# Two of eight depthwise convolution chunks moved from block matmuls to multiply-adds on VectorE

## The chip, the cores and the metric

One core of one Trainium2 chip runs the whole program. The metric is the device time of one execution in microseconds (us); of the kernel before there are three runs, and their median is compared with that of the changed kernel.

## What is computed

One layer of a hybrid decoder, in float32, for 256 prompt positions and 8 samples of 8 new positions (320 columns together, always in this order). The normalised input goes through one input projection (2048 to 3072). A third of its outputs are convolution values, a third are their gates, a third go to a state-space mixer (S5, then gelu and a sigmoid gate). The two mixers' outputs are normalised, projected, added to the input, and a SwiGLU feed-forward follows, then a last norm. The part that the change touches is the convolution of 1024 channels, cut here to its core:

```
u  = v * sigmoid(gate)                        # (b, l, 1024)
up = concatenate([conv_buf, u], axis=1)       # 30 earlier rows in front
y[t, c] = sum over k < 31 of up[t + k, c] * conv_w[k, c]   # each channel by itself
y  = y + conv_b                               # then LayerNorm over channels, swish
new_buf = up[:, -30:]
```

The prompt starts with 30 rows of zeros, each sample with its own 30 rows of state.

## The kernel before

**Weights.** All projections stream their weights in sub-steps of 256 rows by 512 columns. For each sub-step SyncE loads a tile `raw` (four buffers), ScalarE rounds it into `hi` (line 126), VectorE subtracts to get `lo` (line 127), and TensorE does 24 matmuls of 128x320 (lines 150 to 152: four output tiles, two row blocks, three products). `hi` and `lo` have three buffers.

**Order.** The kernel gives every piece of work a number with `when(slot)`: the sub-steps count 0, 1, 2, ..., and other work gets a slot among them, from the table `PLAN`. The framework lists the instructions of each engine in the order in which they become ready in its own simulated timeline, the lowest number first where several are ready, and each engine then runs its list in that order. An instruction that waits on the chip holds all that is behind it on its engine. Sub-steps 0 to 15 project the S5 inputs, 16 to 47 the convolution inputs: groups c0 to c3 of eight sub-steps, each of which gives two chunks of 128 channels, both values and gates. Sub-steps 48 to 55 are the projection `w_glu` of the S5 mixer, whose right side `gehl` comes from the gelu (lines 826 to 834), and this in turn from `yl`, 16 loads on SyncE's queue (line 821). After it come the output projection and the feed-forward.

**A convolution chunk.** When group ci ends, VectorE scales the projected values and gates (lines 915, 920), and writes their product into a window buffer `ubuf` (line 923). There are two such buffers, so that chunk c+2 can be written only when nothing reads chunk c any more. `conv_chunk` (from line 356) then loads the state rows `stn`, moves the samples' new columns (line 363), transposes the state rows on TensorE (line 367) and copies them into the window (ScalarE, line 368), and writes the new convolution state out (lines 370 to 374). After that the window is spread out: four transfers per chunk (line 378) copy it, shifted by 0, 8, 16 and 24 columns, into `ub`, 32 channels and four shifts on the 128 partitions. `conv_weights` (line 352, VectorE) builds block weights `cw` of 128x1024 from the taps. TensorE then does the convolution as 64 products over the prompt's columns (line 386, 128x256) and 64 over the samples' (line 390, 128x64), counted in the trace as instructions, into one PSUM tile `cx`, and ScalarE adds the bias (line 395). `ysum` on VectorE adds the chunk (line 399) for the LayerNorm at slot 62. `stn`, `cw`, `ub` and `cx` have one buffer each.

The slots of the chunks are `P_CONV`; `conv_chunk` is placed 2.2 before its entry and `conv_weights` 2.5 before, and the matmuls at the entry itself. The S5 outputs (`post`, lines 772 to 793) have slots 24 to 34.5, the S5 states 35, the gelu of block b has 44 + b/2.

Of the kernel before, what the change touches and what calls it, by code (L numbers as in the profile page):

```python
# [11 lines left out]
AF = mybir.ActivationFunctionType  # L12
OP = mybir.AluOpType
# [7 lines left out]
ORDER = (("s", 0), ("s", 1), ("c", 0), ("c", 1), ("c", 2), ("c", 3))  # L21
S0, S1 = (8 * ORDER.index(("s", i)) + 8 for i in range(2))
P_POST = [24, 25.5, 27, 28.5, 30, 31.5, 33, 34.5]
P_CONV = [27, 30, 35, 38, 43, 46, 51, 54]
P_GELU = 44
P_LN = 62
E_AT = {2: 0, 3: 1024}
# [12 lines left out]
           + ((("w", b + 2, P_POST[b] + 0.5),) if b < 6 else ())]  # L40
        + [("states", 0, P_POST[7] + 0.5), ("open_g", 0, P_POST[7] + 1)]
        + [("gelu", b, P_GELU + b / 2) for b in range(8)]
        + [("cw", b, P_CONV[b] - 2.5) for b in range(8)]
        + [("conv", b, P_CONV[b] - 2.2) for b in range(8)]
        + [("copy", 0, 65)])
P_RMIX = 0.58
SEQ = ("glu", "ssm", "conv")
# [8 lines left out]
def kernel(ctx: ExitStack, tc: tile.TileContext,  # L56
# [7 lines left out]
    V, A, G, T, SP = nc.vector, nc.scalar, nc.gpsimd, nc.tensor, nc.sync  # L64
# [3 lines left out]
    @contextmanager  # L68
    def when(slot):

        old = tc.cur_priority
        tc.cur_priority = int(BASE + slot * SLOT)
        yield
        tc.cur_priority = old
# [13 lines left out]
    def sx_tile(shape):  # L88
        return pss.tile(shape, F32, tag="sx", name="sx")

    def cx_tile(shape):
        return pss.tile(shape, F32, tag="cx", name="cx", bufs=1)
# [92 lines left out]
    convw = const.tile([128, 8, 32], F32, name="convw")  # L185
    G.memset(convw[:, :, 31:32], 0.0)

    def pv(i):
        return PV[:, i:i + 1]
    NMIX, NFFN, CB, LNG, LNB, GNC, GNS, SSD = 0, 16, 32, 40, 48, 56, 64, 72  # L190
# [6 lines left out]
    convy = convp.tile([128, 8, NTOK], F32, name="convy")  # L197
# [158 lines left out]
    def conv_chunk(c):  # L356
        u = us_.pop(c)
        traced.add(("conv", c))
        stn = convp.tile([120, 2, 128], F32, name="stn", bufs=1)
        SP.dma_start(stn, sc_dram[:, c * 128:(c + 1) * 128]  # L360
                     .rearrange("(h r) c -> r h c", h=2))
        win_ = u[:, 350:654].rearrange("p (b t) -> p b t", t=38)
        A.activation(win_[:, :, 30:38], u[:, 286:350].rearrange("p (b t) -> p b t", t=8), AF.Copy)
        pc = sx_tile([128, 368])
        ps = pc[:, 0:240].rearrange("p (h r) -> p h r", h=2)
        for h in range(2):
            T.transpose(ps[:, h, :], stn[:, h, :], ident[:120, :120])
        A.activation(win_[:, :, 0:30], ps.rearrange("p h (b t) -> p (h b) t", t=30), AF.Copy)
        ps = pc[:94, 240:368]
        T.transpose(ps, u[:, 256:350], ident)  # L370
        uo = convp.tile([94, 128], F32, name="uo", bufs=1)
        A.activation(uo, ps, AF.Copy)
        SP.dma_start(ncv_p[0, 0, :, c * 128:(c + 1) * 128], uo[0:30])
        SP.dma_start(ncv_s[0, :, 22:30, c * 128:(c + 1) * 128], uo[30:94])

        ub = convp.tile([128, 4, UW - 24], F32, name="ub", tag="wide")
        for b in range(4):
            SP.dma_start(ub[:, b, :],  # L378
                         bass.AP(tensor=u.tensor, offset=u[32 * b:32 * b + 32].offset,
                                 ap=[[u.ap[0][0], 32], [8, 4], [1, UW - 24]]))  # L380
        cw = cw_.pop(c)
        with when(P_CONV[c]):
            acc = cx_tile([128, NTOK])
            for k in range(8):
                for b in (3, 2, 1, 0):
                    T.matmul(acc[32 * b:32 * b + 32, 0:256], cw[:, b, k, :], ub[:, b, k:k + 256],  # L386
                             start=(k == 0), stop=False, skip_group_check=True)
            for k in range(8):
                for b in range(4):
                    T.matmul(acc[32 * b:32 * b + 32, 256:320].rearrange("p (b t) -> p b t", t=8),  # L390
                             cw[:, b, k, :],
                             bass.AP(tensor=ub.tensor, offset=ub[:, b, 350 + k:351 + k].offset,
                                     ap=[list(ub.ap[0]), [38, 8], [1, 8]]),
                             start=False, stop=(k == 7), skip_group_check=True)
            A.activation(convy[:, c, :], acc, AF.Identity, bias=pv(CB + c))
        if c == 0:
            V.tensor_copy(ysum, convy[:, 0, :])
        else:
            V.tensor_tensor(ysum, ysum, convy[:, c, :], op=OP.add)


    us = bigp.tile([128, 5248], F32, tag="h20", name="us")
# [325 lines left out]
    def s5_sample_states():  # L728
        assert all(("e", b) in traced for b in range(8))
        for h in range(2):  # L730
            scan_step(*((Sn[:, :, 8 * k:8 * k + 8], st0[:, :, 8 * k:8 * k + 8], *powers(0, k, 8))
                        for k in (2 * h, 2 * h + 1)))
# [428 lines left out]
    def post(b):  # L1161
# [4 lines left out]
    job(n_proj, open_mid)  # L1166
    parts_ = dict(v=pool_v, pre=pre, e=s5_e, w=pool_w, scan=s5_scan, post=post, gelu=gelu,
                  cw=conv_weights, conv=conv_chunk, sample=lambda b: s5_sample_states(),
                  states=lambda b: s5_states(), open_g=lambda b: open_g(),
                  copy=lambda b: SP.dma_start(ncv_s[0, :, 0:22, :], state_conv[0, :, 8:30, :]))  # L1170
# [66 lines left out]
```

## Time and profile before

| | us |
|---|---|
| median of three runs | 1435.41 (1434.61 to 1437.08) |
| the profiled execution | 1432.56 |
| its span, first to last instruction | 1430.8 |
| TensorE busy | 1387.2 (97%) |
| VectorE busy | 793.7 (55%) |
| ScalarE busy | 552.2 (39%) |

"Busy" of TensorE counts from the start of a matmul to its modelled end, and matmuls overlap: one of 128x320 is shown with 0.31 us, while the next starts 0.15 us behind it. So the pitch from start to start tells its cost. The same holds in a small way for VectorE, where the next instruction starts a little before the shown end of the one before. In a timeline row, the bracket at the end is the idle time of the engine ahead of that instruction and what ended it. PEclk is the clock granted to TensorE: 1.00 is 2.4 GHz, 0.50 is 1.2 GHz.

### The profile page before, as it was taken

What the parts mean: (1) busy time and instruction counts of PE and PEld (TensorE: products, weight loads), DVE (VectorE), ACT (ScalarE), POOL (GpSimd) and SP (SyncE); (2) the same over time, 40 slices, a digit from 0 to 9 for tenths busy, and PEclk for the clock granted to TensorE, in tenths of its full rate; (3) what the DMA queues carried; (4) which work ended last, traced back from release to release, by engine and by line L of the source; (5) the groups of instructions that cost most, each with busy time, mean ns of one, the idle gap of its engine ahead of it and who ended that gap; (6) DMA issues with size and microseconds to landing.
All of it is one profiled execution on the core that took longest, in us unless ns stands there. A gap on an engine that the chain in (4) does not pass through costs nothing.

```text
span 1430.8 us, 25250 instructions
## 1 busy us (share of the span) xinstructions
PE 1387.2 (97%) x10482; PEld 1354.9 (95%) x10482; DVE 793.7 (55%) x1400; ACT 552.2 (39%) x805; POOL 30.3 (2%) x61
## 2 busy tenths in 40 slices
PE   9999989799998999999999999999999999999995
PEld 8899978788998999999999999999999999999995
DVE  7778985365887744445434544443444435444465
ACT  7434434354464433333333332333333233332232
POOL 0121000000000000000000000000000000000000
PEclk9999999999999999999999999999999999999997
DMA  9874564966543444544444444445444444454432
GB/s 259 223 156 140 168 187 127 164 180 198 190 148 109 149 142 148 160 148 148 148 151 152 150 152 148 148 148 154 154 149 148 148 149 149 156 180 148 148 133 74
DMA packets 147739, 222.73 MB, mean 156 GB/s; under 512 B 32505, under 2 KB 57657, under 8 KB 147480
## 3 DMA queue, kind: packets, MB, share of 16 engines
q1 hardware_dynamic: 144488, 211.09, 48.5%
q0 software_dynamic: 3136, 10.03, 2.8%
q8 instruction: 82, 1.34, 0.4%
q14 instruction: 33, 0.27, 0.1%
HBM read 201.04 MB, written 10.41 MB: 148 GB/s over the span
## 4 chain that ended last, share of the span: by engine, by line
PE 88%; DMA 4%; DVE 3%; SPq 2%; ACT 2%; issue 1%; ACTq 0%; DVEq 0%
PE mm L151 27%; PE mm L152 27%; PE mm L150 27%; DMA ub<-ubuf 3%; PE cx L386 2%; SPq L378 1%; DMA raw<-in_w_in_dram 1%; DVE lo L127 1%; PE sx L787 1%; PE sx L782 1%; PE sx L689 1%; PE cx L390 0%; DMA yl<-yd 0%; DVE us L705 0%; ACT hi L126 0%
## 5 line engine op out<-in xcount | busy, mean ns | idle before, releaser
L127 DVE TENSOR_TENSOR lo<-raw,hi 128x1024 fp32r<-128x1024 f32 x352 | 430.5, 1223 | 449.9 <-ACT hi L126 449.2
L126 ACT ACTIVATE hi<-raw 128x1024 fp32r<-128x1024 f32 x352 | 372.9, 1060 | 653.2 <-PE mm L151 580.0
L150 PE MATMUL mm<-hn,hi 128*128 128x320 f32 x1408 | 434.8, 309 | 0.0
L151 PE MATMUL mm<-hn,hi 128*128 128x320 f32 x1408 | 434.7, 309 | 0.0
L152 PE MATMUL mm<-hn,lo 128*128 128x320 f32 x1408 | 431.1, 309 | 0.0
L150 PEld LDWEIGHTS mm<-hn,hi 128*128 128x128 f32 x1408 | 264.3, 188 | 0.1
L151 PEld LDWEIGHTS mm<-hn,hi 128*128 128x128 f32 x1408 | 264.3, 188 | 0.0
L152 PEld LDWEIGHTS mm<-hn,lo 128*128 128x128 f32 x1408 | 263.2, 188 | 0.0
L150 PE MATMUL mm<-aout,hi 128*128 128x320 f32 x704 | 217.3, 309 | 0.0
L151 PE MATMUL mm<-aout,hi 128*128 128x320 f32 x704 | 217.1, 309 | 0.0
L152 PE MATMUL mm<-aout,lo 128*128 128x320 f32 x704 | 214.7, 309 | 0.0
L150 PEld LDWEIGHTS mm<-aout,hi 128*128 128x128 f32 x704 | 132.2, 188 | 0.0
L151 PEld LDWEIGHTS mm<-aout,hi 128*128 128x128 f32 x704 | 132.2, 188 | 0.0
L152 PEld LDWEIGHTS mm<-aout,lo 128*128 128x128 f32 x704 | 131.5, 188 | 0.0
L151 PE MATMUL mm<-xhl,hi 128*128 128x320 f32 x384 | 121.2, 318 | 0.5 <-DVE xhl L257 0.5
L152 PE MATMUL mm<-xhl,lo 128*128 128x320 f32 x384 | 121.4, 319 | 0.0
L150 PE MATMUL mm<-xhl,hi 128*128 128x320 f32 x384 | 117.4, 319 | 3.5 <-ACT hi L126 2.7
L150 PEld LDWEIGHTS mm<-xhl,hi 128*128 128x128 f32 x384 | 71.8, 191 | 5.7 <-ACT hi L126 2.9
L151 PEld LDWEIGHTS mm<-xhl,hi 128*128 128x128 f32 x384 | 73.5, 192 | 1.7 <-DVE xhl L257 1.1
L152 PEld LDWEIGHTS mm<-xhl,lo 128*128 128x128 f32 x384 | 73.6, 192 | 1.1 <-issue 0.8
L1051 DVE TENSOR_TENSOR h<-mm,h 128x320 f32<-128x320 f32 x64 | 30.0, 487 | 41.2 <-PE mm L152 41.2
L386 PE MATMUL cx<-ub,cw 128*32 128x256 f32 x512 | 35.0, 382 | 10.9 <-DMA ub<-ubuf 10.9
(312 smaller groups left out, 1346.2 us busy)
## 6 DMA issues: line engine op xcount, KB each, us to landing
raw<-in_w_ffn_gate_dram SPq DMA_DIRECT2D x88, 512.0 KB
raw<-in_w_ffn_up_dram SPq DMA_DIRECT2D x88, 512.0 KB
raw<-in_w_ffn_down_dram SPq DMA_DIRECT2D x88, 512.0 KB
raw<-in_w_in_dram SPq DMA_DIRECT2D x64, 256.0 KB
raw<-in_w_out_dram SPq DMA_DIRECT2D x32, 512.0 KB
ub<-ubuf SPq DMA_DIRECT2D x32, 316.0 KB
raw<-in_w_in_dram SPq DMA_DIRECT2D x16, 512.0 KB
tst<-KTd POOLq DMA_DIRECT2D x8, 512.0 KB, 5.6
```

What stands on the lines that cost most here:

```text
L126: A.activation(hi, src, AF.Copy)
L127: V.tensor_tensor(lo, src, hi.bitcast(F32), op=OP.subtract)
L150: T.matmul(ps, wh, xh, start=(k == 0), stop=False)
L151: T.matmul(ps, wh, xl, start=False, stop=False)
L152: T.matmul(ps, wl, xh, start=False, stop=(k == g.nk - 1))
L378: SP.dma_start(ub[:, b, :], bass.AP(tensor=u.tensor, offset=u[32 * b:32 * b + 32].offset, ap=[[u.ap[0][0], 32], [8, 4], [1, UW - 24]]))
L386: T.matmul(acc[32 * b:32 * b + 32, 0:256], cw[:, b, k, :], ub[:, b, k:k + 256], start=(k == 0), stop=False, skip_group_check=True)
L689: T.matmul(ps[64 * g2:64 * g2 + 64, q, r, :], e[:, q, r, 64 * g2:64 * g2 + 64], uall[:, 8 * b + 2 * q + g2, :], start=True, stop=True)
L782: T.matmul(ps[:, 2 * q:2 * q + 2, :].rearrange("p g j -> p (g j)"), w[:, q, r].rearrange("p t c -> p (t c)"), hbd[:, q, r].rearrange("p g ...
L787: T.matmul(ps[:, g, :], t2[:, g].rearrange("p t c -> p (t c)"), uall[:, 8 * b + g, :], start=False, stop=(g == 7), skip_group_check=True)
L1051: V.tensor_tensor(h[:, n, :], ps, h[:, n, :], op=OP.add)
```

## The change

Chunks 3 and 5 get no block weights, no `ub` and no convolution matmuls. Their window is read where it stands: ScalarE writes the product of tap 0 plus the bias, and VectorE does 30 further multiply-adds in place, each as two instructions, prompt (128x256) and samples (128x64) in turn. Tap k of a chunk has the slot `P_CONV` + 0.2 k. The chunks' entries in `P_CONV` go from 38 to 34 and from 46 to 42, and for them `conv_chunk` is placed at the entry and not 2.2 before it. Loading of the state rows, window, transposes and state outputs stay.

```diff
-P_CONV = [27, 30, 35, 38, 43, 46, 51, 54]
+P_CONV = [27, 30, 35, 34, 43, 42, 51, 54]
+V_CONV = {3: 0.2, 5: 0.2}
...
-        + [("cw", b, P_CONV[b] - 2.5) for b in range(8)]
-        + [("conv", b, P_CONV[b] - 2.2) for b in range(8)]
+        + [("cw", b, P_CONV[b] - 2.5) for b in range(8) if b not in V_CONV]
+        + [("conv", b, P_CONV[b] - (0 if b in V_CONV else 2.2)) for b in range(8)]
...
+        if c in V_CONV:
+            return conv_taps_on_v(c, u, win_)
...
+    def conv_taps_on_v(c, u, win_):
+
+        pairs = [(convy[:, c, 0:256], lambda k: u[:, k:k + 256]),
+                 (convy[:, c, 256:320].rearrange("p (b t) -> p b t", t=8),
+                  lambda k: win_[:, :, k:k + 8])]
+        for dst, src in pairs:
+            A.activation(dst, src(0), AF.Identity, bias=pv(CB + c), scale=convw[:, c, 0:1])
+        for k in range(1, 31):
+            with when(P_CONV[c] + V_CONV[c] * k):
+                for dst, src in pairs:
+                    V.scalar_tensor_tensor(dst, src(k), convw[:, c, k:k + 1], dst,
+                                           op0=OP.mult, op1=OP.add)
+        with when(P_CONV[c] + V_CONV[c] * 31):
+            add_ysum(c)
```

`add_ysum` holds the two lines that add a chunk to `ysum`; the other chunks call it as before.

## Rows read from the trace of the kernel before

**Rows 1.** The page: TensorE's busy time and share of the span; granted clock by slice

```profile
PE 1387.2 (97%) x10482; PEld 1354.9 (95%) x10482; DVE 793.7 (55%) x1400; ACT 552.2 (39%) x805; POOL 30.3 (2%) x61
...
PEclk9999999999999999999999999999999999999997
```

**Rows 2.** The page's chain that ended last: share of the span by engine

```profile
PE 88%; DMA 4%; DVE 3%; SPq 2%; ACT 2%; issue 1%; ACTq 0%; DVEq 0%
```

**Rows 3.** TensorE's waits, 170 to 360 us: total us, times, longest

```profile
PE cx L386 <- DMA ub<-ubuf: 10.9, 7, 3.2
PE sx L370 <- ACT ubuf L368: 5.5, 1, 5.5
```

**Rows 4.** Timeline of TensorE around the convolution of chunks 3 and 5

```profile
266.98 3.69 PE L386 MATMUL cx<-ub,cw 128*32 128x256 f32 x64 [2.03 <-DMA ub<-ubuf]
...
271.55 0.42 PE L367 MATMUL sx<-ident,stn 120*128 120x120 f32 x2
...
271.96 0.30 PE L150 MATMUL mm<-xhl,hi 128*128 128x320 f32 x1
272.11 0.31 PE L151 MATMUL mm<-xhl,hi 128*128 128x320 f32 x1
...
281.39 0.45 PE L370 MATMUL sx<-ident,ubuf 128*94 128x128 f32 x1 [5.45 <-ACT ubuf L368]
...
281.90 0.47 PE L150 MATMUL mm<-xhl,hi 128*128 128x320 f32 x1
...
285.90 0.47 PE L150 MATMUL mm<-xhl,hi 128*128 128x320 f32 x1
286.72 0.40 PE L367 MATMUL sx<-ident,stn 120*128 120x120 f32 x2 [0.35 <-DMA stn<-in_state_conv_dram]
...
307.73 3.68 PE L386 MATMUL cx<-ub,cw 128*32 128x256 f32 x64 [2.25 <-DMA ub<-ubuf]
```

**Rows 5.** Timeline of VectorE: what follows a multiply-add, and when

```profile
125.13 0.33 DVE L662 SCALAR_TENSOR_TENSOR ks<-e,PV,cx 128x128 f32<-128x128 f32 x1
125.38 0.67 DVE L604 TENSOR_TENSOR vw<-pw,Bb 128x512 f32<-128x512 f32 x1
...
410.30 0.55 DVE L891 SCALAR_TENSOR_TENSOR half<-lnt,PV,half 128x320 fp32r<-128x320 f32 x1
410.76 0.49 DVE L959 TENSOR_TENSOR t<-mm,Rs 128x320 f32<-128x320 f32 x1
...
18.78 1.55 DVE L439 SCALAR_TENSOR_TENSOR prm<-prm 128x32 f32<-128x32 f32 x7
```

**Rows 6.** Busy us of PE, PEld, DVE, ACT, POOL, then PEclk, by stretch

```profile
230.00:260.00 30.00, 28.43 (x296) 25.23 (x295) 8.69 (x11) 12.81 (x28) 0.88 (x1) 1.00 0.48 137
260.00:300.00 40.00, 31.77 (x392) 28.12 (x391) 19.74 (x32) 19.01 (x45) 0.00 (x0) 0.91 1.01 194
...
230.00:330.00 100.00, 87.12 (x988) 78.38 (x990) 44.14 (x65) 43.91 (x94) 0.88 (x1) 0.97 0.75 169
```

**Rows 7.** VectorE's waits, 230 to 330 us: total us, times, longest

```profile
DVE cw L352 <- PE cx L390: 21.0, 3, 14.3
...
DVE ubuf L923 <- DMA ub<-ubuf: 4.6, 1, 4.6
```

**Rows 8.** VectorE's groups of instructions, 282 to 302 us: busy us, mean ns

```profile
L832 DVE TENSOR_TENSOR ge<-gz,yl 128x320 f32<-128x320 f32 x8 | 6.0, 774 | 0.0
...
L834 DVE TENSOR_TENSOR gehl<-ge,gehl 128x320 fp32r<-128x320 f32 x8 | 3.9, 497 | 0.0
L829 DVE TENSOR_TENSOR gz<-gsq,yl 128x320 f32<-128x320 f32 x8 | 3.9, 494 | 10.6 <-DMA yl<-yd 9.1 <-ACT gsq L827 1.5
L352 DVE TENSOR_TENSOR cw<-tapw,blkmask 128x1024 f32<-128x1024 f32 x1 | 1.2, 1236 | 0.0
```

**Rows 9.** Timeline of ScalarE behind chunk 3's bias, 270 to 282 us

```profile
280.60 0.47 ACT L826 ACTIVATE gsq<-yl 128x320 f32<-128x320 f32 x1 [8.37 <-DMA yl<-yd]
280.98 0.35 ACT L368 ACTIVATE ubuf<-sx 128x240 f32<-128x240 f32 x1
```

More of the change, by code (lines that the diff above doesn't have):

```diff
@@ L395, in conv_chunk, with add_ysum @@
             A.activation(convy[:, c, :], acc, AF.Identity, bias=pv(CB + c))
+        add_ysum(c)
+    def add_ysum(c):
         if c == 0:
@@ L399, in conv_chunk @@
             V.tensor_tensor(ysum, ysum, convy[:, c, :], op=OP.add)
+    def conv_taps_on_v(c, u, win_):
[10 more added lines that the diff above has]
+        with when(P_CONV[c] + V_CONV[c] * 31):
+            add_ysum(c)
     us = bigp.tile([128, 5248], F32, tag="h20", name="us")
```

## The prediction

> **What bounds the kernel now.** I read the page first: TensorE is busy 97% of the span, VectorE 55%, and the granted clock is at its upper level, 2.4 GHz, in every slice but the last [rows 1]. The chain of waits says the same: 88% of it is TensorE, 4% transfers, 3% VectorE [rows 2]. So the kernel is a stream of matmuls, and what TensorE need not do, or need not wait for, is gained, as long as the rest keeps up. I then looked for the places where the stream breaks. TensorE's waits between 170 and 360 us are two things: 10.9 us, in seven pieces, for the spread window `ub` ahead of convolution matmuls, and one wait of 5.5 us for a copy on ScalarE [rows 3]. TensorE's timeline places them [rows 4]: 2.03 us ahead of chunk 3, 2.25 us ahead of chunk 5, and 5.45 us at 276 to 281.4, after which the matmuls of 128x320 run for a while at 0.267 us from start to start (281.90 to 285.90 is 15 pitches), not at 0.15 as at 271.96: the clock had fallen to 1.2 GHz. The stretch table has the mean of 0.91 there [rows 6].
>
> **TensorE's work that goes.** Chunk 3's matmuls occupy TensorE from 266.98 to 271.55, when the next instruction starts: 4.57 us [rows 4]. Chunk 5's first burst is as long (3.68 us against 3.69), so 4.57 again: 9.14 us together. Nothing replaces this on TensorE, and it is on the bound: gain 9.1.
>
> **Waits that go with it.** The two waits for `ub` directly ahead, 2.03 and 2.25, go too: gain 4.3 [rows 4]. What is late next is only what TensorE needs anyway, `hi` and `lo` of the next sub-step. Their lead is two sub-steps, 2 x 24 matmuls x 0.15 = 7 us, from which a rounding on ScalarE and a subtraction on VectorE, near 1 us each, are to be taken. Four issues on SyncE's queue and four transfers go per chunk as well; TensorE's list of waits has none for weights [rows 3], so I count them at nothing, hidden behind the matmuls.
>
> **What VectorE gets.** Per chunk 30 pairs of multiply-adds, with a per-partition factor. The trace has that form at 128x128: 125.13, next start 125.38, so 0.25 us; and at 128x320: 410.30 to 410.76, 0.46 us [rows 5]. That is 0.21 / 192 = 1.09 ns a column; at 256 columns it makes 0.25 + 128 x 0.00109 = 0.39, at 64 columns 0.25 - 0.07 = 0.18. A pair is 0.57 us, 30 are 17.1, both chunks 34.2 us. Each step needs the one before of its own kind. The one chain of that sort, seven of 128x32, took 1.55 us, 0.22 each, though one alone is shown with under 0.2: with such a wait the pitch is about the full shown length [rows 5]. Prompt and samples in turn put the other instruction into that gap. If nothing were hidden, a pair would be 0.48 + 0.28 (the shown lengths 0.33 and 0.55 put on the same line) = 0.76, and both chunks 46 us. I take 34, since the alternation fits that gap; the upper end stays for the range. The block weights go: 1.2 us each [rows 8], so net +32 us.
>
> The Trainium skill ("VectorE: DVE Perf Modes", section "The DRAIN you can't avoid") says that the next operation does not start until the pipe of the one before is empty, and that one should hold the number of operations down; that speaks against 120 small ones. By the row it is not so in this kernel: the next one started 0.46 us into an operation shown with 0.55 [rows 5]. By the page's sentence the sum would be the 46 us, by the row the 34.
>
> **Is there room?** Between 230 and 330 us VectorE is busy 44.1 of 100 us, between 230 and 260 only 8.7 of 30, between 260 and 300 19.7 of 40 [rows 6]. With the 32 us it would be busy 76 of a stretch that shrinks to 87 us. Chunk 3's steps have slots 34.2 to 40, after nearly all of the S5 outputs; its `conv_chunk` goes from slot 35.8 to 34, ahead of the last S5 output and of the states. So its window should stand near 236, not at 256, and 17 us of steps lie in a stretch with 21 us free, much of it a wait for the weights' buffer `cw` (14.3 us at once [rows 7]) which this chunk no longer makes. Chunk 5's product into `ubuf` waits for the last step of chunk 3; before it waited for the `ub` transfer until 267 (4.6 us [rows 7]), so I count nothing. Chunk 5's steps, slots 42.2 to 48, meet the gelu (44 to 47.5), 13.8 us on VectorE [rows 8]. The stretch 260 to 300 then holds 19.7 + 17.1 - 1.2 = 35.6 of 40 us: full, but not over.
>
> **What I can't size.** (a) The hole at 276: ScalarE stood 8.37 us for `yl` with chunk 4's window copy right behind in its list [rows 9]; both come near in other order once chunk 3 is off SyncE's queue. Its price is 5.45 idle, 16 slow matmuls x 0.12 = 1.9, and 0.35 behind them: 7.7. The change gives back 0 to 7.7; I take 2.6, a third, because `yl` keeps its rank in the table. (b) New stalls: a step standing at the head of VectorE's list holds the `lo` or the PSUM reads behind it. From 0 to what would be left over if chunk 3's steps fell into 260 to 300 as well: 35.6 + 17.1 - 40 = 12.7. I take 2.6, near the lower end, since the stretch row has the room.
>
> **Sum.** 9.1 + 4.3 + 2.6 - 2.6 = 13.4 us off the profiled execution: 1432.6 (span 1430.8 and 1.8 around it) becomes 1419.2. The median of the runs shown is 2.8 above that execution, so I forecast 1422.0 for the median.
>
> **Rivals.**
> 1. *The hole closes too.* For it: its cause is a list order, and the queue ahead of `yl` is shorter by four issues. Against: `yl` has no earlier slot. It would give 9.1 + 4.3 + 7.7 = 21.1 off: 1414; the small waits ahead of other chunks (10.9 - 4.3 [rows 3]) could take it to 1411.
> 2. *The waits move on.* Chunks 4 and 6 find their `ub` late instead, and the gelu comes a little late behind chunk 5's steps; only part of TensorE's 9.1 is gained, 3 to 9: about 1429.
> 3. *VectorE becomes the bound, slower.* VectorE runs its list in order. Its idle time was waits at the head of the list: 21.0 for `cw`, 9.1 for `yl` [rows 7, 8]. If steps are listed behind such waits (chunk 5's start value sits behind the same `yl` wait on ScalarE, for instance), they can't use the idle time and come on top. With 20 of the 32 us on top, `lo` and the gelu slip by 20 and TensorE's 13.4 don't cover it: 1435.4 + 6.6 = 1442. It decides where more than 13.4 of the 32 us find no idle time. Against: 21.0 of those waits are the convolution's own, and two of eight chunks leave it.
> 4. *No change in the sum:* the losses of (b) near their upper end, 12.7, with nothing from (a): 1435.
>
> **How the numbers follow.** Forecast (9 to 17 us off) 0.47; rival 1 0.17; rival 2 0.16; rival 4 0.08; rival 3 0.12. What counts as no change is 0.2%, 2.9 us either side of 1435.4 (1432.5 to 1438.3). Faster 0.47 + 0.17 + 0.16 = 0.80; same 0.08; slower 0.12. The range reaches from rival 1's end, 1411, to 1433.5, which leaves out rival 3 and most of rival 4.
>
> **What would show it.** TensorE's instructions fall by 256 matmuls, and its lists have no `cx` rows for chunks 3 and 5. VectorE's multiply-adds: 60 of 128x256 and 60 of 128x64, pairs 0.57 us apart; at 0.76 the alternation hides nothing. Chunk 3's steps start near 236 and end before 260; if they start past 255, rival 3 is near. TensorE's waits for `ub` fall from seven to about five. The stretch 276 to 288 shows whether the hole and the low clock remain. The prediction is wrong if TensorE waits for `lo`, `gehl` or a PSUM buffer for more than about 5 us in 230 to 330, or if the matmuls behind 360 us don't come some 13 us earlier than before.

## The result, and the profile after

The changed kernel takes 1424.18 us (median of six runs, 1421.42 to 1431.02), the kernel before 1436.14 (six runs beside it). The ratio is 0.9916, 95% interval 0.9896 to 0.9936: 12 us, or 0.84%, faster. The forecast was 1422.0 with a range of 1411 to 1433.5.

The profiled execution of the changed kernel is the slowest of its six runs: 1431.02 us, span 1428.9. That of the kernel before was faster than most of its kind (1432.56; the medians in later comparisons are 1437.5 to 1438.8). The spans of these two differ by only 1.9 us, so both kernels were traced once more (experiments 1 and 5), and the accounts below use both pairs.

The page, answering to [rows 1, 2]: 256 instructions fewer on TensorE, 118 more on VectorE, and the shares of the chain nearly as they were.

```profile
PE 1385.4 (97%) x10226; PEld 1352.4 (95%) x10226; DVE 827.2 (58%) x1518; ACT 554.1 (39%) x807; POOL 30.3 (2%) x61
...
PEclk9999998999999999999999999999999999999998
...
PE 88%; DMA 5%; DVE 2%; SPq 2%; ACT 1%; issue 1%; ACTq 0%; DVEq 0%
```

TensorE's waits between 170 and 360 us, answering to [rows 3] (total us, times, longest):

```profile
PE cx L389 <- DMA ub<-ubuf: 16.0, 6, 4.2
PE mm L153 <- DVE lo L128: 1.4, 3, 0.7
PE mm L152 <- DVE gehl L855: 0.9, 1, 0.9
...
```

The 5.5 us wait for ScalarE's copy into `ubuf` is gone. The wait for `ub` is not smaller but larger, 16.0 against 10.9 us, though two chunks fewer ask for it. TensorE's timeline, answering to [rows 4], shows where (start, length, and in brackets the idle time ahead); it begins with chunk 1:

```profile
217.66 5.36 PE L389 MATMUL cx<-ub,cw 128*32 128x256 f32 x64 [4.10 <-DMA ub<-ubuf]
...
245.21 4.14 PE L389 MATMUL cx<-ub,cw 128*32 128x256 f32 x38 [4.17 <-DMA ub<-ubuf]
...
285.98 5.35 PE L389 MATMUL cx<-ub,cw 128*32 128x256 f32 x64 [3.89 <-DMA ub<-ubuf]
...
330.74 5.34 PE L389 MATMUL cx<-ub,cw 128*32 128x256 f32 x64 [2.51 <-DMA ub<-ubuf]
```

Chunks 1, 2, 4 and 6 each wait 2.5 to 4.2 us, and three bursts of 64 matmuls behind such a wait take 5.34 to 5.36 us. The same chunks in the kernel before (their rows did not stand ahead of the prediction):

```profile
212.99 3.69 PE L386 MATMUL cx<-ub,cw 128*32 128x256 f32 x64 [3.24 <-DMA ub<-ubuf]
...
236.98 1.49 PE L386 MATMUL cx<-ub,cw 128*32 128x256 f32 x20 [1.57 <-DMA ub<-ubuf]
...
291.31 3.70 PE L386 MATMUL cx<-ub,cw 128*32 128x256 f32 x64
...
328.21 3.67 PE L386 MATMUL cx<-ub,cw 128*32 128x256 f32 x64 [0.83 <-DMA ub<-ubuf]
```

So chunk 2 waits 2.6 us longer, chunk 4 3.9 and chunk 6 1.7, against the 4.3 us that chunks 3 and 5 no longer wait. Of chunk 2 SyncE issued the four transfers in one piece in the kernel before:

```profile
226.49 5.18 SPq L378 DMA_DIRECT2D ub<-ubuf  x4
```

In the changed kernel it issued them in two pairs, with a store of S5 outputs, `yd`, between them:

```profile
233.75 1.22 SPq L381 DMA_DIRECT2D ub<-ubuf  x2
235.06 1.87 SPq L814 DMA_DIRECT2D yd<-y  x1
236.98 2.83 SPq L381 DMA_DIRECT2D ub<-ubuf  x2
```

TensorE came to chunk 2 3.7 us behind the end of the last of these issues before (231.67 and 235.41) and 1.2 us behind it after (239.81 and 241.04), and in both its burst began 5.3 to 5.4 us behind that end.

The stretches, answering to [rows 6], with a wider one (busy us of PE, PEld, DVE, ACT, POOL, then PEclk):

```profile
230.00:260.00 30.00, 25.83 (x279) 21.84 (x278) 23.69 (x62) 11.07 (x26) 1.77 (x2) 0.89 0.54 149
260.00:300.00 40.00, 36.11 (x335) 33.95 (x334) 29.98 (x76) 16.59 (x35) 0.00 (x0) 0.96 0.78 159
...
230.00:330.00 100.00, 87.30 (x763) 79.46 (x761) 81.81 (x195) 47.38 (x102) 1.77 (x2) 0.93 0.64 156
210.00:350.00 140.00, 121.79 (x1200) 109.01 (x1202) 108.71 (x251) 63.19 (x131) 3.22 (x4) 0.93 0.62 156
```

The clock gained in 260 to 300 us (0.96 against 0.91) and lost in 230 to 260 (0.89 against 1.00): the break has moved. Over 210 to 350 us it fell from 0.98 to 0.93. VectorE's steps, answering to [rows 5], by form (busy us, mean ns, idle ahead) and in the timeline, where a row of several takes its shape from the first, so that the 25 are both forms in turn:

```profile
L417 DVE SCALAR_TENSOR_TENSOR convy<-ubuf,convw,convy 128x256 f32<-128x256 f32 x60 | 29.2, 487 | 0.1
L417 DVE SCALAR_TENSOR_TENSOR convy<-ubuf,convw,convy 128x64 f32<-128x64 f32 x60 | 17.1, 285 | 2.1 <-ACT convy L413 1.8
...
221.13 0.47 DVE L417 SCALAR_TENSOR_TENSOR convy<-ubuf,convw,convy 128x256 f32<-128x256 f32 x1
...
240.75 2.59 DVE L417 SCALAR_TENSOR_TENSOR convy<-ubuf,convw,convy 128x256 f32<-128x256 f32 x5
244.90 7.39 DVE L417 SCALAR_TENSOR_TENSOR convy<-ubuf,convw,convy 128x64 f32<-128x64 f32 x25 [1.56 <-ACT convy L413]
...
328.77 0.28 DVE L417 SCALAR_TENSOR_TENSOR convy<-ubuf,convw,convy 128x64 f32<-128x64 f32 x1
```

VectorE's waits between 230 and 330 us, answering to [rows 7]:

```profile
DVE gz L850 <- ACT gsq L848: 7.2, 1, 7.2
DVE cw L353 <- PE cx L393: 4.5, 1, 4.5
...
```

**Where the time went.** Up to chunk 1's convolution TensorE's and VectorE's instructions are the same in both kernels, and yet TensorE reached it at 209.75 and 211.34 us (before) and at 213.56 and 213.97 (after). In experiments 2, 4 and 8, again with the same instructions up to there, it was 210.7, 211.8 and 211.1, and in experiment 3, with all eight chunks on TensorE, 213.6, so this is a difference between executions and not the change's. It hides most of the gain in the first pair. So the account starts there and ends with the last matmul of the projections that read `hn`. Its ends are in these rows of that tile, the kernel before ahead (first of the two is the first trace):

```profile
L152 PE MATMUL mm<-hn,lo x1408: 302/309/412, 478.2 to 1267.9; 128*128 128x320 f32 x176
L152 PE MATMUL mm<-hn,lo x1408: 302/309/415, 485.4 to 1275.2; 128*128 128x320 f32 x176
```

And of the changed kernel:

```profile
L153 PE MATMUL mm<-hn,lo x1408: 303/309/310, 476.6 to 1266.4; 128*128 128x320 f32 x176
L153 PE MATMUL mm<-hn,lo x1408: 302/309/310, 474.3 to 1264.1; 128*128 128x320 f32 x176
```

| us | before, first | before, again | after, first | after, again |
|---|---|---|---|---|
| from chunk 1 to the last `hn` matmul | 1058.2 | 1063.9 | 1052.8 | 1050.1 |
| of it idle, waiting for `ub` | 10.3 | 12.7 | 15.3 | 14.5 |
| of it idle, other waits | 11.6 | 11.0 | 4.9 | 7.2 |
| the rest (matmuls, at either clock) | 1036.2 | 1040.2 | 1032.6 | 1028.4 |

The stretch shrank by 5.4 us in the first pair and 13.8 in the second. In both pairs the other waits fell (6.7 and 3.8 us: the hole of 5.5 and 6.4 went, new stalls came), the waits for `ub` rose (5.0 and 1.8), and the rest fell (3.6 and 11.8), where the matmuls that went make 9.1. So the matmuls that stayed took 5.5 us more in the first pair and 2.7 less in the second; that this is the clock alone isn't shown. The mean of the two pairs is 9.6 us, against 12 by the medians.

### The profile page after: what moved, and what is told of

Read it like the earlier page. It is cut to its first block, busy times and chain, and to the rows that moved or that the text cites. A ratio compares the mean times of both kernels' runs of the same rounds, so it can differ in the third digit from the quotient of the medians.

```text
span 1428.9 us, 24831 instructions
## 1 busy us (share of the span) xinstructions
PE 1385.4 (97%) x10226; PEld 1352.4 (95%) x10226; DVE 827.2 (58%) x1518; ACT 554.1 (39%) x807; POOL 30.3 (2%) x61
## 4 chain that ended last, share of the span: by engine, by line
PE 88%; DMA 5%; DVE 2%; SPq 2%; ACT 1%; issue 1%; ACTq 0%; DVEq 0%
PE mm L151 27%; PE mm L152 27%; PE mm L153 27%; DMA ub<-ubuf 2%; PE cx L389 2%; DMA raw<-in_w_in_dram 2%; DVE lo L128 1%; SPq L842 1%; SPq L381 1%; ACT hi L127 1%; PE sx L808 1%; PE sx L710 1%; DMA yl<-yd 0%; DMA stn<-in_state_conv_dram 0%; PE sx L803 0%
```

## The experiments

Each ratio is to the kernel before, run beside it on the same chip, with its 95% interval. T is the stretch of the table above: from TensorE's arrival at chunk 1's convolution to the last `hn` matmul.

**1. The changed kernel again** (no edit), to have a second trace.

> The changed kernel once more, for a second trace beside its first, whose execution (1431.0 us) lay above the median of its runs (1424.2). Theory A (the first trace was behind from the start: its TensorE list is the same as before up to chunk 1's convolution at 213 us, and it reached that point 4.7 us later): ratio 0.991 to 0.993 again, and the new trace reaches chunk 1's convolution at 213 +- 2 us, with a span near 1421. Theory B (the change itself makes the middle slow): the new trace reaches chunk 1's convolution at 217 again and the span is near 1428. Both: TensorE waits for the spread windows ahead of the other six chunks about 16 us in all, more than the 10.9 of before.

Measured: 1427.2 against 1438.34, ratio 0.9919 [0.9899, 0.9939]; the execution traced took 1428.48. TensorE again came late to chunk 1 (burst at 218.09 us, before 212.99), as theory B had it, though the change isn't the cause (see above); T is 1050.1. TensorE's waits, 170 to 360 us:

```profile
PE cx L389 <- DMA ub<-ubuf: 14.7, 6, 4.1
PE mm L153 <- DVE lo L128: 3.2, 3, 2.2
...
```

The gain is the same to 0.03%; the 16.0 for `ub` was no accident of one trace; and the new stalls are 4.6 us here (3.2 for `lo`, 0.7 each for `gehl` and `hi`), 2.3 in the first trace (1.4 and 0.9).

**2. Without the 30 steps.** The kernel leaves the taps 1 to 30 of chunks 3 and 5 out; all else stays.

```diff
-        for k in range(1, 31):
+        for k in range(1, 1):
```

> The changed kernel without the 30 multiply-adds of chunks 3 and 5: only tap 0 and bias are computed for them, so VectorE has 120 instructions less (47 us by the lengths shown). Theory A (VectorE's steps are nearly hidden, term (b) of the sum is 2.6): 2 to 4 us faster than the changed kernel, ratio to before 0.988 to 0.990. Theory B (VectorE is near the bound between 294 and 330 us, since gelu and steps meet there, and TensorE's waits for lo and gehl plus the lower clock behind them are its price): 6 to 10 us faster, ratio 0.984 to 0.987.

Measured: 1428.85, ratio 0.9935 [0.9917, 0.9952]; VectorE's busy time in 210 to 350 us falls from 108.7 to 70.8. The wait for `ub` is 15.9 us in 6 pieces, for `lo` 1.9. Neither theory came true: removing 38 us of VectorE's busy time gains nothing that can be measured. The steps are hidden, and the wait for `ub`, taken together, doesn't come from them.

**3. The order alone.** The kernel before, all eight chunks block matmuls, with chunks 3 and 5 listed where the changed kernel lists them.

```diff
-P_CONV = [27, 30, 35, 38, 43, 46, 51, 54]
+P_CONV = [27, 30, 35, 36.2, 43, 44.2, 51, 54]
```

> The kernel before with chunks 3 and 5 brought forward to the slots that they have in the changed kernel (their loading at 34 and 42, their matmuls at 36.2 and 44.2), all eight chunks as block matmuls. Theory A (the gain is TensorE's 9.1 us of matmuls and the 4.3 us of waits ahead of them): ratio 0.998 to 1.003. Theory C (the new order closes the hole of 5.5 us and its low clock at 276 us, and that is most of the gain): ratio 0.993 to 0.996.

Measured: 1433.55, ratio 0.9972 [0.9961, 0.9982]. The waits:

```profile
PE cx L386 <- DMA ub<-ubuf: 11.3, 7, 3.9
PE sx L367 <- DMA stn<-in_state_conv_dram: 1.7, 1, 1.7
PE sx L370 <- ACT ubuf L368: 1.3, 1, 1.3
```

The hole falls from 5.5 us to 1.3 by the order, without a single multiply-add on VectorE, and that is worth about 4 us: a third of the change's gain, not all of it.

**4. Only chunk 3 on VectorE**, chunk 5 back at its slot.

```diff
-P_CONV = [27, 30, 35, 34, 43, 42, 51, 54]
-V_CONV = {3: 0.2, 5: 0.2}
+P_CONV = [27, 30, 35, 34, 43, 46, 51, 54]
+V_CONV = {3: 0.2}
```

> Only chunk 3 on VectorE, chunk 5 as before (block matmuls, slot 46). Theory A (each chunk brings its 4.6 us of matmuls and 2 us of wait): half the gain, ratio 0.995 to 0.997. Theory B (chunk 5's steps cost what they bring, because they meet the gelu): chunk 3 alone gives at least the whole gain, ratio 0.990 to 0.992.

Measured: 1437.07, ratio 0.9992 [0.998, 1.0005]: no gain, which neither theory expected. The hole is closed, but the wait for `ub` is the largest of all runs:

```profile
PE cx L389 <- DMA ub<-ubuf: 18.9, 7, 4.2
```

**5. The kernel before again** (no edit), one run.

> The kernel before once more, for a second trace: its first traced execution (1432.6) is the fastest of its kind so far, the median of 23 runs is 1438. Theory D (the first trace was ahead by luck in the first 60 us, where all kernels have one order): chunk 1's convolution, which the first trace reached at 213 us, is reached at 215 to 218, and the rest of the list takes the same time as in the first trace within 2 us. Theory E (the middle differs from execution to execution too): the stretch behind it is 3 us or more longer, with clock lows that the first trace did not have.

Measured: 1439.56. T is 1063.9, 5.7 longer than in the first trace: the kernel before, too, can find chunk 1's `ub` over 4 us late and have a burst of 5.35 us behind it. Its waits for `ub` are 13.2 us in 8 pieces, and the hole 6.4.

```profile
215.80 5.35 PE L386 MATMUL cx<-ub,cw 128*32 128x256 f32 x64 [4.46 <-DMA ub<-ubuf]
```

**6. Only chunk 5 on VectorE**, chunk 3 back at its slot.

```diff
-P_CONV = [27, 30, 35, 34, 43, 42, 51, 54]
-V_CONV = {3: 0.2, 5: 0.2}
+P_CONV = [27, 30, 35, 38, 43, 42, 51, 54]
+V_CONV = {5: 0.2}
```

> Only chunk 5 on VectorE (slot 42), chunk 3 as before (block matmuls, slot 38). Chunk 3 alone gave 0.9992. Theory A (each chunk brings its own matmuls and wait): 0.995 to 0.997. Theory F (the sum is not made of chunks: what a chunk gives depends on whether the waits for the spread windows and the late gelu move): with chunk 5 alone 0.991 to 0.994, as the two together, or again 0.998 to 1.001, and the trace has as many us of waits for the windows as the 18.9 of chunk 3 alone, where it is slow.

Measured: 1436.24 against 1437.9, ratio 0.9994 [0.9979, 1.001]: no gain either. The hole stays with chunk 3 at its old place:

```profile
PE cx L389 <- DMA ub<-ubuf: 10.6, 6, 3.5
PE sx L371 <- ACT ubuf L369: 5.4, 1, 5.4
```

Each chunk alone takes 4.57 us of matmuls off TensorE and yields nothing; both together yield 12. So the parts don't add up; experiment 4 keeps its longer waits for `ub`, experiment 6 the hole. But the hole and the waits for `ub` of experiment 6 are no larger than those of the kernel before, so they don't tell where its 4.57 us went. In its trace the bursts of chunks 1 and 6 took 6.24 and 5.33 us, 4.2 us more together than in the first trace of the kernel before (3.69 and 3.67); that this is the whole reason isn't shown.

**7. The changed kernel with its block matmuls listed two slots later**, so that `ub` has longer to land.

```diff
-        with when(P_CONV[c]):
+        with when(P_CONV[c] + 2):
```

> The changed kernel, with the convolution matmuls of the other six chunks two slots later (entry + 2, their loading where it was). Theory G (the 15 to 16 us that TensorE waits for the spread windows, and the low clock in the matmuls behind each wait, are the next bound, because the matmuls are listed before their transfers can have landed): the waits fall under 6 us, ratio to before 0.980 to 0.986. Rival (the waits only move: the windows' single buffer starts the next transfer later too, and the gelu or the LayerNorm comes later): 0.990 to 0.994.

Measured: 1423.49, ratio 0.9894 [0.9875, 0.9914]; the wait for `ub` falls from 16.0 to 8.9 us in 4 pieces, T to 1048.1. The edit halves the wait; the ratio's interval overlaps that of the change alone.

**8. The matmuls back.** The changed kernel, and on TensorE as many matmuls as chunks 3 and 5 had, their result unused. They read the window itself with the identity as weights, so that no transfer comes back with them.

```diff
+        with when(P_CONV[c] + 2.2):
+            acc = cx_tile([128, NTOK])
+            for k in range(8):
+                for b in range(4):
+                    T.matmul(acc[32 * b:32 * b + 32, 0:256], ident[:, 32 * b:32 * b + 32],
+                             u[:, k:k + 256], start=(k == 0), stop=False, skip_group_check=True)
+            for k in range(8):
+                for b in range(4):
+                    T.matmul(acc[32 * b:32 * b + 32, 256:320].rearrange("p (b t) -> p b t", t=8),
+                             ident[:, 32 * b:32 * b + 32], win_[:, :, k:k + 8],
+                             start=False, stop=(k == 7), skip_group_check=True)
```

> The changed kernel plus 128 matmul instructions of the old shapes per moved chunk on TensorE, at the old distance from its loading (slots 36.2 and 44.2), which read the window itself and not a spread copy, so that they wait for no transfer; their result goes into the idle accumulator and is not used. Theory A (TensorE's 4.6 us a chunk are on the path): 8 to 10 us slower than the changed kernel, ratio 0.997 to 1.000. Rival (TensorE waits there anyway, so its work in these places is free): 0 to 4 us slower, 0.992 to 0.995.

Measured: 1440.38 against 1437.9, ratio 1.0012 [0.9999, 1.0025]. The whole gain is gone. Chunk 5's added bursts stand in TensorE's timeline with the length that the removed one had [rows 4]:

```profile
297.75 3.66 PE L413 MATMUL cx<-ubuf,ident 128*32 128x256 f32 x64 [0.49 <-ACT convy L398]
301.23 1.13 PE L417 MATMUL cx<-ubuf,ident 128*32 128x64 f32 x64
```

The waits are much as in the changed kernel, 17.0 us for `ub` in 6 pieces and no hole.

T is 1063.5, 10.7 and 13.4 longer than in the two traces of the changed kernel; the two bursts make 9.1 of it. What the other 2 to 4 us are isn't settled.

**9. The state outputs listed three slots later.** In the changed kernel SyncE issues them ahead of half of chunk 1's `ub` transfers, 1.63 and 1.75 us between the two pairs; its queue:

```profile
204.85 1.23 SPq L381 DMA_DIRECT2D ub<-ubuf  x2
206.17 1.63 SPq L374 DMA_DIRECT2D out_dram<-uo  x1
207.85 1.75 SPq L375 DMA_DIRECT2D out_dram<-uo  x1
209.66 2.60 SPq L381 DMA_DIRECT2D ub<-ubuf  x2
```

```diff
-        SP.dma_start(ncv_p[0, 0, :, c * 128:(c + 1) * 128], uo[0:30])
-        SP.dma_start(ncv_s[0, :, 22:30, c * 128:(c + 1) * 128], uo[30:94])
+        with when(P_CONV[c] + 3):
+            SP.dma_start(ncv_p[0, 0, :, c * 128:(c + 1) * 128], uo[0:30])
+            SP.dma_start(ncv_s[0, :, 22:30, c * 128:(c + 1) * 128], uo[30:94])
```

> The changed kernel, with the two writes of each chunk's convolution state on SyncE's queue three slots behind the chunk's entry, so that they no longer stand between the spread transfers of a chunk (in the changed kernel chunk 1's transfers are issued two and two, with 3.5 us of state writes between). Theory G (the waits for the spread windows, 14.5 to 15.3 us, come from the transfers' late issue): they fall by 3 us or more, ratio to before 0.986 to 0.990. Rival (the transfers' own length and the one buffer set them): the waits stay above 13 us, 0.990 to 0.993.

Measured: 1428.98 against 1438.81, ratio 0.9928 [0.9908, 0.9948]; the wait for `ub` is 13.4 us in 6 pieces. Chunk 1's four `ub` transfers are now issued in one piece from 199.95 us on, and the outputs behind them; chunk 1 waits 1.30 us (4.10 in the first trace of the changed kernel) and chunk 4 1.54 (3.89), but chunk 2 still 4.28 and chunk 7 now 3.28 (0.68). The waits shorten by 1.3 to 2.6 us together, those for `hi` and `lo` make 4.8, and nothing measurable is gained.

**10. Both edits of experiments 7 and 9** on the changed kernel.

> Both edits together: state writes three slots behind the entry, convolution matmuls of the six chunks two slots behind it. Theory G: TensorE waits for the windows under 6 us and the clock stays up behind them, ratio 0.982 to 0.988, faster than either edit alone. Rival (what the windows no longer cost comes back at the LayerNorm, which then stands behind chunk 7): 0.989 to 0.992.

Measured: 1421.74 against 1438.81, ratio 0.9878 [0.9857, 0.99]: the lowest of all, clear of experiment 9 beside it (1428.98), not clear of experiment 7. TensorE's waits, 170 to 360 us, and then the stretch 210 to 350 us:

```profile
PE mm L151 <- issue: 3.5, 1, 3.5
PE cx L390 <- DMA ub<-ubuf: 3.1, 2, 1.7
...
```

```profile
210.00:350.00 140.00, 132.86 (x1345) 116.83 (x1343) 115.24 (x273) 66.84 (x142) 3.94 (x6) 0.98 0.66 179
```

The waits for `ub` are 3.1 us, the clock of 210 to 350 us is back at 0.98 from 0.93, and T is 1043.5, 6.6 to 9.3 shorter than the changed kernel's two. The waits for `ub` fell by more than that, 11.6 to 12.9 us; part of it came back as one wait of 3.5 us for nothing that the profile shows.

**11. A third chunk.** Experiment 10 with chunk 7 on VectorE too.

```diff
-P_CONV = [27, 30, 35, 34, 43, 42, 51, 54]
-V_CONV = {3: 0.2, 5: 0.2}
+P_CONV = [27, 30, 35, 34, 43, 42, 51, 50]
+V_CONV = {3: 0.2, 5: 0.2, 7: 0.2}
```

> The same with chunk 7 on VectorE too (slot 50, taps 0.2 apart). Theory A with VectorE still free enough: TensorE loses another 4.6 us of matmuls and one wait, 4 to 7 us faster than the kernel with both edits. Rival (VectorE is the bound by then: chunk 7's steps fall among the gated outputs and the LayerNorm waits for the last of them): 0 to 10 us slower than it, and TensorE waits for lo, PSUM reads or the LayerNorm's statistics.

Measured: 1424.15, ratio 0.9889 [0.9869, 0.9909]: no better than two. TensorE now waits 5.5 us for the statistics `rg` of the norm of the S5 mixer's outputs, against 4.57 us of matmuls removed. Their small steps on VectorE stand among chunk 7's multiply-adds and take from 345.00 to 354.08 us; in experiment 10 they took from 338.41 to 341.40.

```profile
PE sx L300 <- DVE rg L292: 5.5, 1, 5.5
...
```

**12. The two edits without the change**: the kernel before with the edits of 7 and 9.

> The kernel before (all eight chunks as block matmuls) with the two edits on the order: state writes three slots behind the entry, convolution matmuls two slots behind it. With the change these edits gave 0.988, the change alone 0.992. Theory A (the change's gain is TensorE's 9.1 us, whatever the waits do): about 0.994 to 0.997, so that the change on top of them is still worth 0.6 to 0.9%. Rival (the gain of the change was mostly waits that better order removes too): 0.988 to 0.991, within 0.2% of the changed kernel with both edits.

Measured: 1437.2 against 1437.48, ratio 0.999 [0.9977, 1.0002]. The waits, here from 170 to 520 us:

```profile
PE sx L370 <- ACT ubuf L368: 7.3, 1, 7.3
PE cx L387 <- DMA ub<-ubuf: 5.8, 4, 2.1
```

The wait for `ub` halves (from 10.9 and 13.2) and the hole grows (from 5.5 and 6.4): no gain. The hole takes back less than the waits for `ub` give; TensorE's busy time in T is 1047.2 us here, against 1036.1 and 1040.1 in the kernel before, and why isn't settled. Experiment 10's ratio over this one, 0.9878 / 0.999, is 0.989: on top of the two edits the change is worth some 16 us. The matmuls that go (9.1) and the hole that is gone in experiment 10 (7.3) would make 16.4.

## Why the prediction was right, step by step

The sum of 13.4 us stands against 12 measured, and TensorE's work carries it as forecast. Behind the sum stand two steps that went wrong in opposite directions, the waits for `ub` and the hole; that their errors offset each other in part is luck.

1. *TensorE's work that goes, 9.1 us:* right, and shown to be needed for the gain. Experiment 8 gives TensorE this work back and little else (one of the bursts waits 0.49 us for ScalarE), and the gain is gone. But it is worth its length only where nothing grows in its place: taken one chunk at a time (experiments 4 and 6) it bought nothing.
2. *Waits that go with it, 4.3 us:* this step failed. "The two waits for `ub` directly ahead, 2.03 and 2.25, go too": the two went, but those of chunks 2, 4 and 6 grew by more, and all together rose from 10.9 in seven pieces (13.2 in eight when traced again) to 16.0 and 14.7 in six, where 10.9 - 4.3 in about five was forecast. Instead of 4.3 gained, 1.8 to 5.0 us were lost by the account. That is rival 2's mechanism, and it names the chunks 4 and 6. What I didn't reckon with is where matmuls and transfers would then stand to each other. Counted from its arrival at chunk 1, TensorE came to chunk 4 13.0 us sooner in the first pair of traces and to chunk 6 3.0 us sooner, with less to do and no hole: it arrives ahead of the transfers. To chunk 2 it came 1.8 us later, and the transfers came later still: their last issue ended 4.3 us later by the same count (SyncE's rows in the section on the result). Experiments 7, 9 and 10 show that the place of matmuls and transfers in the lists sets the wait (16.0, then 8.9, 13.4 and 3.1), and experiment 2 that VectorE's steps don't, taken together. Experiment 8, with the matmuls back, keeps 17.0 us of it: there too the issues for chunk 2 stand in two pairs; they end 24.7 us behind TensorE's arrival at chunk 1 (21.9 in the first trace before), and chunk 2 waits 3.57. So the earlier arrival alone can't be the cause; what its other waits come from is open. Chunk 1's wait is no part of it: 3.24 and 4.46 before, 4.10 and 4.12 after.
3. *What VectorE gets, 34 us hidden:* the durations were right: 487 and 285 ns shown, against 0.48 and 0.28; 25 instructions in turn take 7.39 us, so 0.59 a pair against 0.57. They are hidden (experiment 2). The place was wrong in part. Chunk 3's prompt steps began at 221.13 us, not near 236, with no sample steps between them, since the samples' start value on ScalarE came only ahead of 244.90; the last prompt step ended at 259.4, but the last sample step at 272.1, not before 260, and chunk 5's ended at 329. Chunk 5's product into `ubuf` didn't wait for the last of them, as the prediction had it: VectorE wrote it at 266.94, when only the sample steps were left. Part of that was a head-of-list wait of rival 3's kind: 4.5 us for `cw` until chunk 2's matmuls were done, with chunk 3's steps behind it. VectorE was busy 81.8 of the 100 us from 230 to 330, forecast 76, which was still room enough.

   The Trainium skill ("VectorE: DVE Perf Modes", section "The DRAIN you can't avoid") speaks of each operation waiting until the pipe of the one before is empty, and of an earlier start for one that nothing holds. In the 25 steps in turn the trace agrees with the second: 0.59 a pair, where the shown lengths add up to 0.77. Steps of one kind, each needing the one before, stand at 2.59 / 5 = 0.52 us, no shorter than their shown 0.49; there the trace agrees with the first.
4. *(a) The hole at 276 us, taken as 2.6 of 7.7:* too low. It closed in every kernel that listed chunk 3 at the new place, nearly so in experiment 3 (1.3 left), and stayed (5.4 to 7.3) in every one with chunk 3 at the old place: the kernel before, experiments 5, 6 and 12. So it was the list order, as argued, and of rival 1 this half came true. The low clock behind it did not go for good: it is behind the waits for `ub` now.
5. *(b) New stalls, taken as 2.6 of 12.7:* right in size, 2.3 us in the first trace and 4.6 in the second, for `lo`, `gehl` and `hi`. The gelu came late as feared, its last `gehl` at 320.4 us, but TensorE waited 0.9 us for it.

The signs to watch said some of this: the instruction count (10482 to 10226) and the pair's length were met, `ub` missed on the wrong side, and the matmuls behind were not 13 us earlier in the first pair of traces (1266.4 against 1267.9) but 11.1 earlier in the second (1264.1 against 1275.2). A pair of single traces can hide most of a gain of 0.8%; the medians can't.

## What to carry to other kernels

Work taken off the bounding engine is worth its length only if the transfers that it meets next are early enough: price the waits that remain, since they may grow as the engine arrives sooner or as their transfers are issued later. Before crediting a change, undo its order and its work apart from each other: here the order alone gave 4 us, the matmuls put back lost the whole gain, and half the change (either chunk) gave nothing. When engines list their work by slots, where a consumer and its transfers stand in the lists is worth a trial of its own, with the change and without: the same two edits gave nothing to the kernel before, and some 5 us on top of the change, the best of all, at 0.9878.

## What the runs showed of the hardware that was not expected

A short wait can cost TensorE more than its length. Behind waits of 4.10, 3.89 and 2.51 us the burst of 64 matmuls took 5.34 to 5.36 us instead of 3.69, 1.7 us more each. The granted clock at the start of these three bursts, for chunks 1, 4 and 6 (PE, PEld, DVE, ACT, POOL, then PEclk), had fallen from the upper level, 2.4 GHz, to the lower, 1.2 GHz, for all or most of the 2 us:

```profile
217.70:219.70 2.00, 2.00 (x24) 1.26 (x28) 2.00 (x6) 0.76 (x2) 0.00 (x0) 0.61 0.31 109
...
286.00:288.00 2.00, 2.00 (x24) 1.36 (x28) 1.34 (x5) 0.00 (x0) 0.00 (x0) 0.60 1.11 291
331.00:333.00 2.00, 2.00 (x24) 1.18 (x20) 1.93 (x5) 1.66 (x5) 0.00 (x0) 0.50 0.78 278
```

The length of the wait alone doesn't decide: in the kernel before, chunk 1's burst behind 3.24 us ran in 3.69, and so did chunk 4's behind 3.01 us in the second trace of the changed kernel:

```profile
285.17 3.69 PE L389 MATMUL cx<-ub,cw 128*32 128x256 f32 x64 [3.01 <-DMA ub<-ubuf]
```

The Trainium skill ("TensorE: Matmul & The Clock Gate", section "HAM oscillation — how this bites in real kernels") tells the same of another kernel: a wait for a transfer ahead of each group of matmuls sets the clock back, and each group starts cold. This case's trace agrees for the three bursts, at 1.7 us each, and not for the two that ran in 3.69; and experiment 10, whose waits are short, has the clock of 210 to 350 us at 0.98, not 0.93.

And single executions of one kernel differ ahead of anything that was changed: TensorE came to chunk 1's convolution between 209.75 and 213.97 us in kernels whose TensorE and VectorE do the same up to there, and T of the kernel before was 5.7 us apart in its two traces.
